# Shift products of two modulated norms: the shift held still, rounded weights of two tiles moved past it

## The chip, the cores and the metric

The kernel runs on one core of a Trainium2 chip (trn2). The time is device time in microseconds for one execution of the whole program, from its first to its last instruction on the core, as the median of the executions shown.

## What is computed

The reference runs two blocks, one behind the other, on a sequence of 512 rows with 1,024 features. The first has four layers: forgetting attention, a state-space layer, a multi-scale pool and again forgetting attention, each with a gated feed-forward net (SwiGLU). The second block has two layers with a mixer that joins attention and a state-space scan, and again a SwiGLU net. What the change touches is how the second block normalizes:

```
mod = (silu(c) @ w_ada[l] + b_ada[l])[:, None, :]
sh1, sc1, g1, sh2, sc2, g2 = jnp.split(mod, N_MOD, axis=-1)
h = rmsnorm(x, norm1_w[l]) * (1.0 + sc1) + sh1
x = x + g1 * hybrid_mixer(h, ...)
h = rmsnorm(x, norm2_w[l]) * (1.0 + sc2) + sh2
x = x + g2 * swiglu_2(h, w_gate_up[l], w_down[l])
```

So a product `h @ W` behind such a norm has two parts: the scaled `x` times `W`, which needs a factor for each row (the reciprocal root of the mean square), and the shift `sh` times `W`, one number for each column of `W`, the same for all rows.

## The kernel before

Activations are kept with the features on the partitions: `x` is eight tiles (`KD`) of 128 features x 512 rows. A weight tile is 128 x 128 and is the stationary operand, 512 rows move past it. Each fp32 value is split into two roundings of the type fp32r, a high and a low part (`Xh`, `Xl` for activations, `wh`, `wl` for weights), and a product is three matmuls: high by high, and the two mixed ones (`p3`, L265).

**Weights.** They lie in HBM in the order of use, eight tiles to a chunk of 128 x 1024. `pump` (L200) loads a chunk into `wraw` (four buffers, SyncE's queue), ScalarE rounds it into `wh` (three buffers, L174) and VectorE makes `wl` (two buffers, L181). `wnext(n, ...)` (L231) hands out the next n tiles of the current chunk; `raw_w` (L252) gives the unrounded fp32 tile.

**The order of work.** Each engine runs its instructions in an order that is laid down when the program is built: an instruction is placed when the model of the machine used there has its inputs and its buffers ready, those written first in the program going first. `keep_in_program_order` holds an instruction behind what was written before it for the same engine. Tiles of one tag share a fixed number of buffers.

**The modulation.** In the background of earlier layers the vector `mod` (128 x 96, both layers and all six parts) is made, and from it the gains `acol`; `end` (L1475) closes that work. `Ada` (L1493) is one modulated norm. There are four: the two mixers (`mixer`) and the two feed-forward nets (`feed`), in the order mixer 0, feed 0, mixer 1, feed 1. They are called lead 1 to lead 4 below.

**The lead** (L1537). The root of the mean square isn't known yet when a stage begins, so its first two weight tiles for each k, i = 0 and 1, are multiplied with `x` times gain, without the row factor, into `pld` (three matmuls each). Behind each of these, one fp32 product of the raw weight tile with one column, the shift, goes into `psh`; the two `psh` take both buffers of the PSUM tag `sc`. At k = 1 and k = 4 the sums of squares (`pc`, L401) and the row factors (`nps`, L411) are put in. At the end ScalarE copies the two columns into `adb` (`b`), and for every k VectorE makes `sqt` (x times gain times row factor; two buffers), ScalarE rounds `sqt` plus the shift into the new `Xh`, and VectorE makes the new `Xl`.

**Behind the lead** the other products use these new tiles: in the feed-forward net (`ffn7`, L670) the loop over k for `pgu`, in the mixer (`hybrid`, L1623) the loop for `pk` and `pm`, two weight tiles for each k. Only then is `pld` closed: times the row factor, plus `b`.

Of the kernel before, what the change touches and what calls it, by code (L numbers as in the profile page):

```python
# [20 lines left out]
P = 128  # L21
# [47 lines left out]
def kernel(  # L69
# [179 lines left out]
        pump(i)  # L249
        return hs[i], ls[i]  # L250

    def raw_w():  # L252

        c, o = divmod(st["slot"] - 1, SLOTS)
        return raws[c][:, o * P:(o + 1) * P]

    def walign(n):
        while st["slot"] % n:
            keys.append(None)
            st["slot"] += 1  # L260

    def mm(o, l, r, s0, s1, onto=False):
        pe.matmul(o, lhsT=l, rhs=r, start=s0, stop=s1, skip_group_check=onto)  # L263

    def p3(o, l, r, first, last, onto=False):  # L265
        mm(o, l[0], r[0], first, False, onto)
# [166 lines left out]
    def ffn(name_gu, name_dn, lay, deferred, post, nbg=3, lead=None, ada=None):  # L433
        with tc.tile_pool(name="ffn", bufs=1, reuse_waits="tile") as fp:
            ph = fp.tile([P, KF, S], F32R, name="ph")
            F0 = 3
            plo = [fp.tile([P, F0, S], F32R, name="pl0")]
            R = {}

            def pl(f):  # L440
                if f >= F0 and len(plo) == 1:
                    plo.append(fp.tile([P, KF - F0, S], F32R, name="pl1", tag="pl1", bufs=1))
                return plo[0][:, f, :] if f < F0 else plo[1][:, f - F0, :]

            def tmp():
                return fp.tile([P, S], F32, name="t1", tag="t1", bufs=3)

            def close(f, pg, pu):
                t_ = tmp()
                if deferred:  # L450
                    v.tensor_tensor(out=t_, in0=pg, in1=R["r"], op=ALU.mult)  # L451
                    a.activation(t_, t_, AF.Silu)
                    v.tensor_tensor(out=t_, in0=pu, in1=t_, op=ALU.mult)  # L453
                    g_.tensor_tensor(out=t_, in0=t_, in1=R["r"], op=ALU.mult)  # L454
                else:
                    a.activation(t_, pg, AF.Silu)
                    v.tensor_tensor(out=t_, in0=pu, in1=t_, op=ALU.mult)
                keep(f, t_)

            def keep(f, t_):  # L460
                a.activation(ph[:, f, :], t_, AF.Copy)
                v.tensor_tensor(out=pl(f), in0=t_, in1=ph[:, f, :].bitcast(F32), op=ALU.subtract)
                bgstep(nbg)

            def gu_key(which, f, k):
                return ("t", name_gu, lay, k * P, which * DFF + f * P)

            def gu(t, which, f, k):
                p3(t, wnext(1, gu_key(which, f, k)), xk(k), k == 0, k == KD - 1)

            f0 = 0
            if ada:
                f0 = 2
                (pg, pu), r, b = ada.lead([lambda k, i=i: gu_key(i, 0, k) for i in range(2)])
                pp = [acc("pgu") for _ in range(2)]
                for k in range(KD):
                    for i, t in enumerate(pp):
                        gu(t, i, 1, k)
                t_, tu = tmp(), tmp()
                tt(t_, pg, r, ALU.mult)  # L480
                a.activation(t_, t_, AF.Silu, bias=b[:, 0:1])
                tt(tu, pu, r, ALU.mult)
                stt(t_, tu, b[:, 1:2], t_, ALU.add, ALU.mult)
                keep(0, t_)
                close(1, *pp)
            if lead:

                f0 = F0
                steps = lead(fp.tile([P, (KF - F0) * S], F32, name="lroom", tag="pl1", bufs=1), tmp)
                pp = [(acc if i < 4 else scp)("pgu") for i in range(2 * f0)]  # L490
                for k in range(KD):
                    steps[k]()
                    for i, t in enumerate(pp):
                        gu(t, i % 2, i // 2, k)
                        if (k, i) == (KD - 1, 3):
                            rc = rstd_cols(nrm["sq"])
                R["r"] = keep_rstd(rstd_rows(rc))
                for f in range(f0):
                    close(f, pp[2 * f], pp[2 * f + 1])
            for f in range(f0, KF):  # L500
                pg, pu = acc("pg"), acc("pu")
                for which, t in enumerate((pg, pu)):
                    for k in range(KD):
                        gu(t, which, f, k)
                    if deferred and "c" not in R and not lead:
                        R["c"] = rstd_cols(nrm["sq"])
                    elif deferred and "r" not in R:
                        R["r"] = keep_rstd(rstd_rows(R["c"]))
                close(f, pg, pu)
            for m in range(KD):  # L510
                po = acc("po")
                for f in range(KF):
                    w = wnext(1, ("t", name_dn, lay, f * P, m * P))
                    p3(po, w, (ph[:, f, :], pl(f)), f == 0, f == KF - 1)
                post(m, po)
                bgstep(nbg)

    def ffn7(name_gu, name_dn, lay, deferred, upd, fin, nbg=3, ada=None, plain=(0,)):
# [4 lines left out]
        with tc.tile_pool(name="ffn", bufs=1, reuse_waits="tile") as fp:  # L523
# [41 lines left out]
            def gu_key(which, f, k):  # L565
                return ("t", name_gu, lay, k * P, which * DFF + f * P)
# [100 lines left out]
            f0 = 0  # L667
            if ada:
                f0 = 2
                (pg, pu), r, b = ada.lead([lambda k, i=i: gu_key(i, 0, k) for i in range(2)])  # L670
                pp = [acc("pgu") for _ in range(2)]
                for k in range(KD):
                    for i, t in enumerate(pp):
                        gu(t, i, 1, k)
                t_, tu = tmp(), tmp()
                tt(t_, pg, r, ALU.mult)
                a.activation(t_, t_, AF.Silu, bias=b[:, 0:1])
                tt(tu, pu, r, ALU.mult)
                stt(t_, tu, b[:, 1:2], t_, ALU.add, ALU.mult)
                keep(0, t_)  # L680
                close(1, *pp)
# [759 lines left out]


    mod = cp.tile([P, 96], F32, name="mod")
    acol = cp.tile([P, 32], F32, name="acol")

    def modc(lay, which, k):
# [3 lines left out]
    def ada_thunks(bp):  # L1450
# [24 lines left out]
        def end():  # L1475
            p2 = part.rearrange("p (i two) -> p two i", two=2)
            tt(mod, p2[:, 0], p2[:, 1], ALU.add)
            at, n_ = COLS["b_ada"]
            tt(mod, mod, cols[:, at:at + n_], ALU.add)
            for lay in range(2):  # L1480
                for i, nm in ((0, "n1"), (1, "n2")):
                    at, _ = COLS[nm]
                    sc = mod[:, lay * 48 + (1 + 3 * i) * 8:lay * 48 + (1 + 3 * i) * 8 + 8]
                    o = acol[:, lay * 16 + i * 8:lay * 16 + i * 8 + 8]
                    stt(o, sc, 1.0, cols[:, at + lay * 8:at + lay * 8 + 8], ALU.add, ALU.mult)
            at, n_ = COLS["fin_g"]
            tt(facol, acol[:, 0:KD], cols[:, at:at + n_], ALU.mult)

        return [start, act] + [lambda i=i: step(i) for i in range(192)] + [end] + rope_thunks(bp, T)
# [3 lines left out]
    class Ada:  # L1493
# [42 lines left out]

        def lead(self, keyf):  # L1537
            pp = [acc("pld") for _ in range(2)]
            pb = [scp("psh") for _ in range(2)]
            for k in range(KD):  # L1540
                for i in range(2):
                    w = wnext(1, keyf[i](k))
                    p3(pp[i], w, xk(k), k == 0, k == KD - 1)
                    mm(pb[i][:, 0:1], raw_w(), self.shift(k), k == 0, k == KD - 1)
                if k == AT_C:
                    rc = self.cols()
                if k == AT_R:
                    r = rstd_rows(rc)
            b = nsmall("adb", 2, 2)
            for i in range(2):  # L1550
                a.activation(b[:, i:i + 1], pb[i][:, 0:1], AF.Copy)
            for k in range(KD):
                xh, xl = new_X(k)
                u_ = ntile("sqt", 2)
                stt(u_, x[:, k, :], self.gain(k), r, ALU.mult, ALU.mult)
                a.activation(xh, u_, AF.Identity, bias=self.shift(k))
                stt(xl, u_, self.shift(k), xh.bitcast(F32), ALU.add, ALU.subtract)
            return pp, keep_rstd(r), b

        def final_x(self, k):  # L1560
            if k == 0:
# [30 lines left out]
    def hybrid(lay, post, ada):  # L1592
        W = "w_in_2"
        with tc.tile_pool(name="hyb", bufs=1, reuse_waits="tile") as fp:
# [25 lines left out]

            sql = []
            keyf = [lambda k, i=i: ("t", W, lay, k * P, i * P) for i in range(3)]
            pq, r, b = ada.lead(keyf[:2])  # L1623
            pk, pm = acc("pa"), acc("pm")
            for k in range(KD):
                p3(pk, wnext(1, keyf[2](k)), xk(k), k == 0, k == KD - 1)
                w = wnext(1, ("c", W, lay, k * P, ((0, 384, 32), (32, 1952, 8))))
                p3(pm[:64], [t_[:, :64] for t_ in w], xk(k), k == 0, k == KD - 1)
            for i in range(3):
                wcol = col("qa_w", 2 * lay + i) if i < 2 else col("kva_w", lay)  # L1630
                h_, l_ = (qn[0][:, i, :], qn[1][:, i, :]) if i < 2 else kvn
# [585 lines left out]
```

## Time and profile before

| | |
|---|---|
| median of 3 executions | 3480.41 us (3479.81 to 3483.42) |
| profiled execution, its own time | 3482.38 us |
| span of the profiled execution | 3480.6 us |
| TensorE (PE) matmul busy | 3412.9 us, 98% of the span |
| TensorE weight loads (PEld) busy | 2908.2 us, 84% |
| VectorE (DVE) busy | 2337.6 us, 67% |
| ScalarE (ACT) busy | 1486.0 us, 43% |
| GpSimd (POOL) busy | 486.6 us, 14% |
| mean granted TensorE clock | 0.992 |

Times in the trace count from the start of the span. Matmuls are pipelined: the record of one is longer than the spacing to the next, so what one costs in a stream is read from the distance between starts. Weight loads have records of their own. A row with x2 is two instructions merged; what stands in brackets is how long the engine stood idle before the row, and what it was released by. The lines of the code are given as L263 and the like; nearly all matmuls are issued by the helper in line 263, so they are told apart by the names of their tiles.

### The profile page before, as it was taken

The numbers are of one execution on the slowest core, as the hardware profiler recorded it, in microseconds if no ns is written. First come the engines' busy times: TensorE is split into PE (matmuls) and PEld (weight loads), VectorE is DVE, ScalarE is ACT, GpSimd is POOL, SyncE is SP. The second block draws the span as 40 slices with busy tenths as digits, with TensorE's granted clock in tenths as the row PEclk, the third lists the DMA queues.
The fourth block names the chain that finished last, engine by engine and source line by source line (L and its number), as shares of the span: only waits on it lengthen the run. The fifth ranks groups of instructions, "written<-read, shape, count | busy, mean of one in ns | idle before, by whom it ended". The sixth has DMA issues, their size and how long they took to land.

```text
span 3480.6 us, 49473 instructions
## 1 busy us (share of the span) xinstructions
PE 3412.9 (98%) x18620; PEld 2908.2 (84%) x18620; DVE 2337.6 (67%) x4335; ACT 1486.0 (43%) x2419; POOL 486.6 (14%) x597
## 2 busy tenths in 40 slices
PE   8999999989999989999999999999999999999999
PEld 6888778878888868888788989988889998788998
DVE  8876786355555576555676866876686677658666
ACT  4554333314433233322455633556553356645333
POOL 1003443011111021101000100132110002211000
PEclk9999999999999999999999999999999999999999
DMA  5423344474455434554422232321122232113232
GB/s 155 110 70 98 117 138 139 140 251 136 131 169 169 152 106 160 169 168 146 136 73 70 92 103 97 106 80 55 37 95 100 97 110 83 48 41 106 85 110 97
DMA packets 189167, 395.56 MB, mean 114 GB/s; under 512 B 57552, under 2 KB 84320, under 8 KB 186880
## 3 DMA queue, kind: packets, MB, share of 16 engines
q1 hardware_dynamic: 186592, 375.61, 33.3%
q10 hardware_dynamic: 2304, 16.78, 1.4%
q8 instruction: 146, 2.39, 0.3%
q14 instruction: 93, 0.76, 0.1%
q0 software_dynamic: 32, 0.02, 0.0%
HBM read 372.33 MB, written 24.20 MB: 114 GB/s over the span
## 4 chain that ended last, share of the span: by engine, by line
PE 70%; DVE 5%; ACT 2%; issue 1%; DMA 1%; POOL 1%; POOLq 0%; SPq 0%; DVEq 0%; ACTq 0%
PE po L263 20%; PE qa L263 9%; PE pu L263 8%; PE pg L263 7%; PE qc L263 7%; PE pgl L263 2%; PE px L263 2%; PE pq L263 2%; PE pv L263 2%; PE sc L263 2%; PE pld L263 1%; PE pz L263 1%; DVE wl L181 1%; PE tp L753 1%; PE pV L263 1%
## 5 line engine op out<-in xcount | busy, mean ns | idle before, releaser
L174 ACT ACTIVATE wh<-wraw 128x1024 fp32r<-128x1024 f32 x514 | 542.7, 1057 | 676.8 <-PE po L263 339.5
L181 DVE TENSOR_TENSOR wl<-wraw,wh 128x1024 fp32r<-128x1024 f32 x433 | 546.1, 1262 | 278.7 <-issue 81.2
L263 PE MATMUL po<-ph,wl 128*128 128x512 f32 x1056 | 411.0, 389 | 1.0 <-DVE wl L181 1.0
L263 PE MATMUL po<-ph,wh 128*128 128x512 f32 x1056 | 411.2, 390 | 0.0
L263 PE MATMUL po<-pl,wh 128*128 128x512 f32 x1056 | 411.0, 389 | 0.0
L390 POOL TENSOR_TENSOR sqa<-sqa,sqt 128x512 f32<-128x512 f32 x72 | 112.1, 1557 | 1390.3 <-ACT sqt L389 1389.7
L263 PE MATMUL pu<-Xh,wh 128*128 128x512 f32 x632 | 248.4, 393 | 0.0
L263 PE MATMUL pu<-Xh,wl 128*128 128x512 f32 x632 | 247.6, 392 | 0.6 <-DVE wl L181 0.6
L263 PE MATMUL pu<-Xl,wh 128*128 128x512 f32 x632 | 247.8, 392 | 0.2 <-DVE Xl L399 0.2
L263 PE MATMUL qa<-T,wh 128*128 128x256 f32 x1296 | 236.9, 283 | 0.0
L263 PEld LDWEIGHTS po<-ph,wl 128*128 128x128 f32 x1056 | 198.3, 188 | 42.8 <-DVE wl L181 1.4
L263 PEld LDWEIGHTS po<-pl,wh 128*128 128x128 f32 x1056 | 198.3, 188 | 41.2 <-DVE pl L551 0.4
L263 PEld LDWEIGHTS po<-ph,wh 128*128 128x128 f32 x1056 | 198.3, 188 | 41.0 <-issue 0.4
L263 PE MATMUL pg<-Xh,wh 128*128 128x512 f32 x568 | 223.7, 394 | 1.4 <-DVE t L451 1.4
L263 PE MATMUL pg<-Xl,wh 128*128 128x512 f32 x568 | 221.9, 391 | 0.0
L263 PE MATMUL pg<-Xh,wl 128*128 128x512 f32 x568 | 221.4, 390 | 0.0
L263 PEld LDWEIGHTS qa<-T,wh 128*128 128x128 f32 x1296 | 202.2, 192 | 0.0
L263 PE MATMUL qa<-T,wsl 128*128 128x256 f32 x648 | 183.8, 284 | 2.6 <-DVE wsl L181 2.6
L174 ACT ACTIVATE wh<-ws 128x1024 fp32r<-128x1024 f32 x108 | 114.4, 1059 | 151.6 <-PE po L263 48.4
L1471 DVE SCALAR_TENSOR_TENSOR adaj<-adaw,cbc 128x512 bf16<-128x512 f32 x192 | 143.7, 749 | 47.0 <-DMA adaw<-in_wada_dram 46.5
L181 DVE TENSOR_TENSOR wsl<-ws,wh 128x1024 fp32r<-128x1024 f32 x108 | 131.9, 1231 | 32.8 <-ACT wh L174 32.3
L454 POOL TENSOR_TENSOR t<-t,rstd 128x512 f32<-128x512 f32 x66 | 86.7, 1315 | 474.3 <-DVE t L453 471.6
(565 smaller groups left out, 8228.5 us busy)
## 6 DMA issues: line engine op xcount, KB each, us to landing
wraw<-in_wst_dram SPq DMA_DIRECT2D x541, 512.0 KB, 3.4
adaw<-in_wada_dram SPq DMA_DIRECT2D x192, 256.0 KB, 3.1
cbc<-c_d SPq DMA_DIRECT2D x32, 256.0 KB, 3.3
tbbr<-br_d ACTq DMA_DIRECT2D x8, 1024.0 KB, 5.5
tbct<-ct_d ACTq DMA_DIRECT2D x8, 1024.0 KB, 5.2
ct_d<-s5cp SPq DMA_DIRECT2D x128, 32.0 KB, 1.9
br_d<-s5ev SPq DMA_DIRECT2D x32, 128.0 KB, 2.0
ct_d<-kp_d SPq DMA_DIRECT2D x32, 128.0 KB, 2.8
```

The lines of the kernel that those rows point to most:

```text
L174: a.activation(hs[i], whole(i), AF.Copy)
L181: v.tensor_tensor(out=ls[i], in0=whole(i), in1=hs[i].bitcast(F32), op=ALU.subtract)
L263: pe.matmul(o, lhsT=l, rhs=r, start=s0, stop=s1, skip_group_check=onto)
L390: (v if m == KD - 1 else g_).tensor_tensor(out=nrm[key], in0=nrm[key], in1=q, op=ALU.add)
L454: g_.tensor_tensor(out=t_, in0=t_, in1=R["r"], op=ALU.mult)
L753: pe.transpose(t_[:, j * P:(j + 1) * P], pr[:, j * P:(j + 1) * P], ident)
L1471: tc.keep_in_program_order(v.scalar_tensor_tensor(out=j, in0=T.pop(i), scalar=1.0, in1=T["c"][:, (i % 2) * W:(i % 2) * W + W], op0=ALU.mul ...
```

## The change

The shift itself is split into two roundings, once, into `mods` (128 x 96 x 2). In the lead both weight tiles of a k are now taken together (`wnext(2, ...)`, with `walign(2)` ahead so that both lie in one chunk). The pair of roundings of the shift for this k, 128 x 2, becomes the stationary operand, and the rounded weights of the two tiles move past it, 256 columns at a time: once `wh`, once `wl`, all summed in the first two partitions of a single `psh`. The sum over the two partitions for each column is the shift product, but it lies along a row. It is copied into a buffer of the tag `sqt` (`rows_`), and `bias` turns it: two fp32 products, each with 2 x 128 values of `rows_` as the stationary operand and a column of two ones moving, into `psb`, then one copy into `adb`. `bias` is called behind k = 1 of the next loop, and its two products are held in that place by `here`. `raw_w` goes away.

```
+    mods = cp.tile([P, 96, 2], F32R, name="mods")
...
+            a.activation(mods[:, :, 0], mod, AF.Copy)
+            tt(mods[:, :, 1], mod, mods[:, :, 0].bitcast(F32), ALU.subtract)
...
         def lead(self, keyf):
             pp = [acc("pld") for _ in range(2)]
-            pb = [scp("psh") for _ in range(2)]
+
+            pb = scp("psh")
+            walign(2)
             for k in range(KD):
+                w = wnext(2, *[f_(k) for f_ in keyf])
                 for i in range(2):
-                    w = wnext(1, keyf[i](k))
-                    p3(pp[i], w, xk(k), k == 0, k == KD - 1)
-                    mm(pb[i][:, 0:1], raw_w(), self.shift(k), k == 0, k == KD - 1)
+                    p3(pp[i], tuple(t[:, i * P:(i + 1) * P] for t in w), xk(k), k == 0, k == KD - 1)
+                at = self.lay * 48 + self.i * 24 + k
+                for i in range(2):
+                    mm(pb[0:2, 0:2 * P], mods[:, at, :], w[i], k == 0 and i == 0, k == KD - 1 and i == 1)
                 if k == AT_C:
                     rc = self.cols()
                 if k == AT_R:
                     r = rstd_rows(rc)
             b = nsmall("adb", 2, 2)
-            for i in range(2):
-                a.activation(b[:, i:i + 1], pb[i][:, 0:1], AF.Copy)
+            rows_ = ntile("sqt", 2)
+            a.activation(rows_[0:2, 0:2 * P], pb[0:2, 0:2 * P], AF.Copy)
+
+            def bias():
+                p_ = scp("psb")
+                for i in range(2):
+                    here(mm(p_[:, i:i + 1], rows_[0:2, i * P:(i + 1) * P], ones[0:2, 0:1], True, True))
+                a.activation(b, p_[:, 0:2], AF.Copy)
+                return b
+
...
-            return pp, keep_rstd(r), b
+            return pp, keep_rstd(r), bias
```

In `ffn7` and `hybrid` the loop over k behind the lead gets, the same in both:

```
+                    if k == 1:
+                        b = bias()
```

New helpers are `here`, which is `tc.keep_in_program_order`, and `mm` now returns its instruction.

## Rows read from the trace of the kernel before

**Rows 1.** The page: busy time of TensorE, and the chain that ended last.
```profile
PE 3412.9 (98%) x18620; PEld 2908.2 (84%) x18620; DVE 2337.6 (67%) x4335; ACT 1486.0 (43%) x2419; POOL 486.6 (14%) x597
...
PE 70%; DVE 5%; ACT 2%; issue 1%; DMA 1%; POOL 1%; POOLq 0%; SPq 0%; DVEq 0%; ACTq 0%
```

**Rows 2.** View of the tile psh: record lengths min/median/max in ns, first and last start.
```profile
L263 PEld LDWEIGHTS psh<-mod,wraw x128: 187/188/338, 2269.6 to 3138.3; 128*128 128x128 f32 x128
L263 PE MATMUL psh<-mod,wraw x128: 164/228/353, 2269.8 to 3138.3; 128*128 128x1 f32 x128
L1551 ACT ACTIVATE adb<-psh x8: 152/171/172, 2290.2 to 3138.6; 128x1 f32<-128x1 f32 x8
```

**Rows 3.** Timeline of TensorE, lead 4 and behind it: start us, length us.
```profile
3122.06 0.39 PE L263 MATMUL pld<-Xh,wh 128*128 128x512 f32 x1
...
3122.74 0.28 PE L263 MATMUL psh<-mod,wraw 128*128 128x1 f32 x2
...
3132.93 0.47 PE L263 MATMUL pld<-Xh,wh 128*128 128x512 f32 x1
...
3138.42 0.48 PE L263 MATMUL pgu<-Xh,wh 128*128 128x512 f32 x1
...
3149.96 0.39 PE L263 MATMUL pg<-Xh,wh 128*128 128x512 f32 x1
```

**Rows 4.** Timeline, 256-column products in the feed-forward net behind lead 2.
```profile
2576.62 0.28 PE L263 MATMUL qc<-T,wsl 128*128 128x256 f32 x1
...
2578.05 0.28 PE L263 MATMUL qc<-T,wsl 128*128 128x256 f32 x1
```

**Rows 5.** Timeline of VectorE and ScalarE, end of lead 4 and behind it.
```profile
3133.21 1.41 DVE L281 SCALAR_TENSOR_TENSOR sqt<-x,acol,nps 128x512 f32<-128x512 f32 x2 [1.73 <-PE nps L263]
...
3133.99 1.38 ACT L1556 ACTIVATE Xh<-sqt,mod 128x512 fp32r<-128x512 f32 x2 [2.90 <-DVE sqt L281]
...
3134.75 1.42 DVE L281 SCALAR_TENSOR_TENSOR Xl<-sqt,mod,Xh 128x512 fp32r<-128x512 f32 x2
...
3136.08 1.40 DVE L281 SCALAR_TENSOR_TENSOR sqt<-x,acol,nps 128x512 f32<-128x512 f32 x2
...
3137.68 0.17 ACT L1551 ACTIVATE adb<-psh 128x1 f32<-128x1 f32 x1 [2.31 <-PE psh L263]
...
3138.49 1.22 DVE L181 TENSOR_TENSOR wl<-wraw,wh 128x1024 fp32r<-128x1024 f32 x1 [1.00 <-PE pld L263]
...
3139.63 1.49 DVE L281 SCALAR_TENSOR_TENSOR Xl<-sqt,mod,Xh 128x512 fp32r<-128x512 f32 x2
...
3141.03 1.40 DVE L281 SCALAR_TENSOR_TENSOR sqt<-x,acol,nps 128x512 f32<-128x512 f32 x2
...
3142.95 1.41 DVE L281 SCALAR_TENSOR_TENSOR Xl<-sqt,mod,Xh 128x512 fp32r<-128x512 f32 x2
```

**Rows 6.** Timeline of TensorE behind lead 4: two matmuls that waited.
```profile
3147.53 0.50 PE L263 MATMUL pgu<-Xl,wh 128*128 128x512 f32 x1 [0.22 <-DVE Xl L281]
...
3176.21 0.39 PE L263 MATMUL qc<-T,wsl 128*128 128x256 f32 x1 [1.22 <-DVE wsl L181]
```

**Rows 7.** One stretch of lead 1: length, busy us of PE, PEld, DVE, ACT, POOL, granted clock, DMA.
```profile
2276.30:2283.00 6.70, 6.70 (x22) 5.64 (x22) 0.72 (x1) 1.47 (x3) 1.17 (x4) 0.51 0.00 0
```

**Rows 8.** Timeline of TensorE in lead 1, at and behind the sums of squares.
```profile
2274.09 1.05 PE L263 MATMUL pc<-ones,sqa 128*128 128x1 f32 x8 [1.26 <-DVE sqa L390]
...
2275.55 0.95 PE L263 MATMUL pc<-ones,sq2a 128*128 128x1 f32 x8
...
2277.20 0.77 PE L263 MATMUL pld<-Xh,wh 128*128 128x512 f32 x1
...
2278.62 0.42 PE L263 MATMUL psh<-mod,wraw 128*128 128x1 f32 x2
2278.90 0.77 PE L263 MATMUL pld<-Xh,wh 128*128 128x512 f32 x1
```

**Rows 9.** View of the tile p1g: a ScalarE copy of 256 columns out of PSUM.
```profile
L638 ACT ACTIVATE p1g<-qa x27: 358/383/387, 1949.8 to 3425.2; 128x256 f32<-128x256 f32 x27
```

More of the change, by code (lines that the diff above doesn't have):

```diff
@@ L250, in quad_next @@
         return hs[i], ls[i]
-    def raw_w():
-        c, o = divmod(st["slot"] - 1, SLOTS)
-        return raws[c][:, o * P:(o + 1) * P]
     def walign(n):
@@ L262, in mm, with here @@
     def mm(o, l, r, s0, s1, onto=False):
-        pe.matmul(o, lhsT=l, rhs=r, start=s0, stop=s1, skip_group_check=onto)
+        return pe.matmul(o, lhsT=l, rhs=r, start=s0, stop=s1, skip_group_check=onto)
+    def here(ins):
+        return tc.keep_in_program_order(ins)
     def p3(o, l, r, first, last, onto=False):
@@ L473, in ffn @@
                 f0 = 2
-                (pg, pu), r, b = ada.lead([lambda k, i=i: gu_key(i, 0, k) for i in range(2)])
+                (pg, pu), r, bias = ada.lead([lambda k, i=i: gu_key(i, 0, k) for i in range(2)])
                 pp = [acc("pgu") for _ in range(2)]
@@ L669, in ffn7 @@
                 f0 = 2
-                (pg, pu), r, b = ada.lead([lambda k, i=i: gu_key(i, 0, k) for i in range(2)])
+                (pg, pu), r, bias = ada.lead([lambda k, i=i: gu_key(i, 0, k) for i in range(2)])
                 pp = [acc("pgu") for _ in range(2)]
@@ L674, in ffn7 @@
                         gu(t, i, 1, k)
+                    if k == 1:
+                        b = bias()
                 t_, tu = tmp(), tmp()
@@ L1622, in hybrid @@
             keyf = [lambda k, i=i: ("t", W, lay, k * P, i * P) for i in range(3)]
-            pq, r, b = ada.lead(keyf[:2])
+            pq, r, bias = ada.lead(keyf[:2])
             pk, pm = acc("pa"), acc("pm")
@@ L1628, in hybrid @@
                 p3(pm[:64], [t_[:, :64] for t_ in w], xk(k), k == 0, k == KD - 1)
+                if k == 1:
+                    b = bias()
             for i in range(3):
```

## The prediction

> **What bounds the kernel now.** I read the page first. TensorE is busy 98% of the span and makes up 70% of the chain that ended last [rows 1], so a matmul taken away normally gives its time back; the question is where something else ends last. The view of the tile `psh` then shows the whole of what is changed: 64 fp32 products recorded as 128 weight loads and 128 one-column matmuls, spread over four leads, and eight small copies into `adb` [rows 2]. Next comes TensorE in order of time through one lead (lead 4, the last feed-forward one). The reader is to see two spacings there: 0.68 us for the three 512-column products of a weight tile, and 0.915 us from one tile to the next [rows 3]. Then VectorE in the same lead, which makes the new `Xh`, `Xl` for the loop behind it [rows 5], and the places further on where TensorE waits for VectorE [rows 6]. Leads 2 and 3 repeat lead 4's spacings; lead 1 is different [rows 7, 8].
>
> **What a shift product costs.** Six tiles of lead 4, from 3132.93 to 3138.42, take 5.49 us, so 0.915 us each. Three 512-column matmuls take 0.68 us (3122.06 to 3122.74). The shift product is the rest, 0.235 us, and 16 of them make 3.76 us of a lead [rows 3].
>
> **What takes its place.** For every tile there is one 256-column product with a two-column stationary operand. No row has that stationary width. The nearest rows are 256-column products with full 128-column weights: twelve of them from 2576.62 to 2578.05, 0.119 us each [rows 4]. Upper bound: 0.119 us, since narrower weights can't load slower. Lower bound: half of a 512-column spacing of 0.227 us, 0.113 us. I take 0.119. Per lead, 16 x (0.235 - 0.119) = 1.86 us is saved; by the lower bound it would be 1.95 us.
>
> The Trainium skill (TensorE: Matmul & The Clock Gate, section Back-to-back issue gap) gives the isolated gap at full clock as N/2.4 + 2.5 ns, which is an estimate of 109 ns for 256 columns. The rows have 119 ns for that width, so the page's figure is below what this kernel shows; by it a lead would save 2.0 us instead of 1.86.
>
> **Lead 1.** Here TensorE is through its first four tiles at 2272.83 and then waits 1.26 us for VectorE's last square [rows 8]. The four tiles become 0.47 us faster and the wait 0.47 us longer: nothing gained. Behind it the clock is granted at 0.51, the lower of its two levels (1.2 of 2.4 GHz), for 6.7 us [rows 7]; a tile takes 1.70 us there, 2277.20 to 2278.90, of which the shift product's record is 0.42 us [rows 8]. Twice 0.119 us, an estimate, replaces that, leaving 1.52 us. Twelve tiles remain: before, 6.7 us hold 3.94 of them and 8.06 follow at 0.915, 14.07 us; after, 6.7 us hold 4.41 and 7.59 follow at 0.80, 12.77 us. Lead 1 saves 1.30 us if the clock does the same again.
>
> Gross: 1.30 + 3 x 1.86 = 6.88 us.
>
> **Does the saving get past VectorE?** Behind a lead VectorE ends last. In lead 4 it makes four `sqt` and two `Xl` by 3137.49, stands still 1.00 us until the lead's last `pld` lets go of a `wl` buffer, makes `wl` at 3138.49, and then runs `Xl` and `sqt` without a break [rows 5]; TensorE catches up with it at 3147.53 [rows 6]. So that run starts with the end of the lead, and an earlier end moves all of it forward, as long as VectorE's idle 1.00 us isn't used up. The six tiles behind `nps` shorten by 6 x 0.116 = 0.70 us, so it is not. What shifts the other way: the last reader of that `wl` buffer used to be `pld`, with the copy starting 0.07 us behind the lead's end (3138.49 against 3138.42). Now it is the last shift product. A 256-column matmul's record is about 0.28 us long and starts 0.12 us before the end, so `wl` starts about 0.2 us behind it. That is 0.13 us for each lead, 0.5 us in all.
>
> **The turn of the rows.** ScalarE copies 2x256 values out of PSUM (a 128x256 copy takes 0.383 us [rows 9]; of the two small copies of 0.17 us one goes away [rows 2]), and two fp32 products with one column turn them, pinned behind the k = 1 products of the next loop. A `psh` product is the same form with more rows: 0.235 us each, 0.47 us for a lead, at least 0.28 us by the length of its record alone. The loop behind lead 4 is 48 products of 0.227 us, 10.88 us, but takes from 3138.42 to 3149.96, 11.54 us, as TensorE meets VectorE's late `Xl` [rows 3, 6]. Those 0.66 us cover the 0.47; with the cover gone it would cost 4 x 0.47 = 1.9 us. Behind lead 4 a longer wait for `wsl` follows, 1.22 us [rows 6], a second cover. Behind the pinned turn the whole product stream waits, so its input must be early: TensorE reaches it 12 products, 2.72 us, behind the lead.
>
> **The borrowed buffer.** The rows lie in one of the two `sqt` buffers, which VectorE's run needs in pairs [rows 5]. In lead 4 both hold values when the lead ends, and the first comes free with the first `Xl` behind `wl`, about 2.1 us later (3139.63 plus 0.75, and the 0.13 from above). Then the copy (0.38 us) ends near 2.5 us, the turn runs from 2.72 to 3.2 us, and the second `sqt` of the next pair, wanted at 3.3 us behind the lead's end (3141.03 plus one of two steps), just finds its buffer. I charge 0.1 us a lead, 0.4 us in all; if each pair missed by a full 0.7 us step it would be 2.8 us.
>
> **The rest.** `mods` adds one copy and one subtraction of 96 columns, once, each at most the 0.383 us of 256 columns [rows 9], under TensorE's work in the second attention; uncovered, 0.8 us. Raw weight buffers come free earlier, as no product reads them: that changes when loads start, and no wait for `wraw` stands in the leads' chain. There are no new transfers, and `walign(2)` adds no padding where slots are even.
>
> Sum: 6.88 - 0.5 - 0.4 = 6.0 us. The profiled execution took 3482.38 us, so 3476.4 us; it stands 2.0 us above the median of the runs shown, 3480.41, so the forecast for a median is 3474.4 us. A measurement of this kernel can tell about 0.2%, 7.0 us; the forecast is just inside that.
>
> **The rivals.**
> *The borrowed buffer holds up VectorE.* If the rows take their buffer before the run of `sqt` begins, each `sqt`, `Xh`, `Xl` goes one after the other: from 3133.21 to the end of the first `Xl`, 0.71 us behind 3134.75, is 2.25 us, against 1.41 us for a step in pairs [rows 5]. It holds until the turn, about 7.8 us in all, 3.5 steps instead of 5.5, less the idle 1.00 us: some 1.5 us a lead, 6 us, which eats the gain: 3480 us. For it: the rows are written down ahead of the run. Against: their copy can't be ready before the lead ends, and today's `adb` copy, written down ahead too, runs at 3137.68, behind the first `Xh` at 3133.99 [rows 5].
> *TensorE stands at the turn (the other side).* If the copy gets its buffer only when the next pair's first `Xl` is done (3142.95 plus 0.71, 5.2 us behind the lead [rows 5]), the pinned turn would stop TensorE from 2.72 to 5.6 us, 2.9 us a lead; less the 0.66 us cover, 9 us over four, against 6.4 gained: 3483 us, and up to 3489 if the 1.22 us wait for `wsl` [rows 6] grows in each lead too. It decides from 2.2 us of standing a lead, 6.0 / 4 + 0.66. Against it: a turn that is late when the order is laid down can be placed behind later products, as only earlier ones are pinned ahead of it.
> *The clock.* The low clock in lead 1 comes behind the 1.26 us wait and 16 one-column matmuls [rows 7, 8]. Denser products might keep it at full: 6.7 us at half speed give back about 3.3 us, 3471 us. The wait grows by 0.47 us, which speaks for no change or worse (another 3.3 us, near 3478 us).
> The Trainium skill (TensorE: Matmul & The Clock Gate, section Why this matters for your kernels) asks that idle gaps between bursts of matmuls be kept short; by that the longer wait speaks against the change, and the low clock behind the wait agrees with it.
>
> **How the numbers follow.** Forecast 0.60; buffer 0.16; TensorE at the turn 0.10; clock regained 0.14. The forecast's own range is 3472 to 3478 us, by the unknown widths (+0.4), the turn's cover (-1.9), the buffer (-2.4) and 2 us by which runs differ. The threshold is 3473.4 us: of the forecast about a third lies below it, of the regained clock nearly all, 0.33 faster. Slower needs 3487.4 us: a third of the turn rival, and an order downstream that comes out badly, 0.07. The rest, 0.60, is within 0.2%. The range of 3469.5 to 3481.5 us leaves out the far ends of the clock and the turn.
>
> **What would show it.** No `psh` record with one column; 64 of 128x256 with a 0.119 us spacing; tiles 0.80 us apart; leads of 14.5 us instead of 16.36 (3122.06 to 3138.42); `wl` 0.2 us behind a lead's end; the turn inside the next loop, which stays at about 11.5 us. Wrong would be: a TensorE wait ended by ScalarE's copy ahead of the turn, `sqt` going singly, or a change in the stretches between leads, where nothing is edited and only the order could differ.

## The result, and the profile after

The changed kernel takes 3505.7 us in the median (3499.4 to 3509.7, 6 executions); the kernel before took 3478.2 us on the same chip (3473.2 to 3483.4, 6). The ratio on record is 1.007, 95% interval [1.006, 1.0079]; the two medians alone give 1.0079. The forecast was 3474.4 us and the range ended at 3481.5: the change was to gain 6 us and loses 27.5 by the medians. The profiled execution after has a span of 3503.7 us, 23.1 us more than that of before.

The page of the kernel after shows nothing of it: TensorE's busy share and the head of the chain that ended last are those of [rows 1].

```profile
PE 3421.9 (98%) x18572; PEld 2899.6 (83%) x18572; DVE 2338.4 (67%) x4336; ACT 1489.5 (43%) x2420; POOL 481.3 (14%) x597
...
PE 70%; DVE 5%; ACT 2%; DMA 1%; issue 1%; POOL 1%; SPq 0%; DVEq 0%; ACTq 0%; POOLq 0%
```

The tile `psh` after, which answers to [rows 2]: 64 products with 256 columns and two-column weights in place of 64 recorded in 128 pieces, and one copy of 2 x 256 for each lead.

```profile
L258 PEld LDWEIGHTS psh<-wh,mods x32: 82/83/123, 2273.1 to 3155.3; 128*2 128x2 f32 x32
L258 PE MATMUL psh<-wh,mods x32: 277/280/345, 2273.3 to 3155.6; 128*2 128x256 f32 x32
...
L258 PE MATMUL psh<-wl,mods x32: 276/281/285, 2273.4 to 3155.7; 128*2 128x256 f32 x32
L1561 ACT ACTIVATE sqt<-psh x4: 357/357/358, 2292.2 to 3156.8; 2x256 f32<-2x256 f32 x4
```

TensorE in order of time at the end of lead 4, after; it answers to [rows 3] and [rows 6].

```profile
3154.18 0.39 PE L258 MATMUL pld<-Xh,wh 128*128 128x512 f32 x1
...
3155.57 0.28 PE L258 MATMUL psh<-wh,mods 128*2 128x256 f32 x1
3155.68 0.28 PE L258 MATMUL psh<-wl,mods 128*2 128x256 f32 x1
3158.75 1.06 PE L258 MATMUL pgu<-Xh,wh 128*128 128x512 f32 x2 [2.79 <-ACT Xh L1574]
...
3165.45 0.50 PE L258 MATMUL pgu<-Xl,wh 128*128 128x512 f32 x1 [0.84 <-DVE Xl L280]
...
3168.75 0.73 PE L258 MATMUL pgu<-Xh,wh 128*128 128x512 f32 x2 [0.71 <-ACT Xh L1574]
...
3170.07 0.50 PE L258 MATMUL pgu<-Xl,wh 128*128 128x512 f32 x1 [0.59 <-DVE Xl L280]
...
3174.22 0.50 PE L258 MATMUL pgu<-Xl,wh 128*128 128x512 f32 x1 [0.96 <-DVE Xl L280]
...
3176.60 0.39 PE L258 MATMUL pg<-Xh,wh 128*128 128x512 f32 x1
```

The products are as cheap as forecast: two tiles and their two shift products, 3154.18 to 3155.80 by the spacing of 0.12, take 1.62 us, 0.81 us a tile where it was 0.915. But behind the lead TensorE stands for 2.79 us, waits again and again for `Xh` and `Xl`, and the loop that took 11.54 us takes 17.85 (3158.75 to 3176.60). VectorE and ScalarE at the same place, after, which answers to [rows 5]:

```profile
3156.06 1.23 DVE L181 TENSOR_TENSOR wl<-wraw,wh 128x1024 fp32r<-128x1024 f32 x1 [6.23 <-PE psh L258]
3156.85 0.36 ACT L1561 ACTIVATE sqt<-psh 2x256 f32<-2x256 f32 x1
3157.20 0.74 DVE L280 SCALAR_TENSOR_TENSOR sqt<-x,acol,nps 128x512 f32<-128x512 f32 x1
3157.98 0.72 ACT L1574 ACTIVATE Xh<-sqt,mod 128x512 fp32r<-128x512 f32 x1 [0.77 <-DVE sqt L280]
3158.73 0.75 DVE L280 SCALAR_TENSOR_TENSOR Xl<-sqt,mod,Xh 128x512 fp32r<-128x512 f32 x1 [0.79 <-ACT Xh L1574]
...
3159.52 0.75 DVE L280 SCALAR_TENSOR_TENSOR sqt<-x,acol,nps 128x512 f32<-128x512 f32 x1
...
3163.35 0.60 PE L258 MATMUL psb<-ones,sqt 2*128 2x1 f32 x4
...
3163.99 0.17 ACT L1567 ACTIVATE adb<-psb 128x2 f32<-128x2 f32 x1 [0.45 <-PE psb L258]
3163.99 0.75 DVE L280 SCALAR_TENSOR_TENSOR sqt<-x,acol,nps 128x512 f32<-128x512 f32 x1 [0.61 <-PE psb L258]
```

Before, the first two `sqt` began at 3133.21, 5.2 us ahead of the lead's end [rows 5]. Now VectorE does nothing for the last 6.23 us of the lead; the first `sqt` comes at 3157.20, 1.2 us behind the record of the last shift product (3155.68 plus 0.28), and then one `sqt`, one `Xh`, one `Xl` take turns until the turn of the rows gives back the second buffer at 3163.99. The granted clock pays too. The windows of the same stretch (length; busy time of PE, PEld, DVE, ACT, POOL; granted clock; DMA):

```profile
3155.97:3158.75 2.78, 0.00 (x0) 0.00 (x0) 1.90 (x3) 1.96 (x3) 0.00 (x0) 1.00 0.19 31
3158.75:3161.75 3.00, 3.00 (x7) 2.12 (x8) 2.93 (x5) 0.72 (x1) 0.00 (x0) 0.54 0.38 146
3161.75:3176.60 14.85, 11.74 (x46) 7.84 (x45) 13.51 (x21) 8.81 (x13) 1.91 (x2) 0.98 0.11 35
```

In the 3.0 us behind the 2.79 us of standing the clock is granted at 0.54, near the lower of its two levels (1.2 of 2.4 GHz). The Trainium skill (TensorE: Matmul & The Clock Gate, section Why this matters for your kernels) asks that idle gaps between bursts of matmuls be kept short. The trace agrees in that the low clock comes behind the stand, though this stand of 2.79 us is shorter than the gaps that the page warns of.

The four leads side by side, from TensorE's starts: a lead from its first `pld` to the first product of the loop behind it, and that loop up to the first product of what follows. All in us, one profiled execution each; the last five rows are experiments below.

| | lead 1, loop | lead 2, loop | lead 3, loop | lead 4, loop | sum |
|---|---|---|---|---|---|
| before | 21.84, 12.33 | 16.36, 11.53 | 16.36, 11.49 | 16.36, 11.54 | 117.8 |
| after | 22.09, 16.68 | 18.40, 17.68 | 17.72, 16.03 | 18.40, 17.85 | 144.8 |
| own tile | 19.17, 11.75 | 15.49, 11.68 | 14.77, 11.75 | 15.44, 11.66 | 111.7 |
| rows behind the run | 19.17, 11.68 | 15.44, 11.66 | 14.77, 11.68 | 15.47, 11.71 | 111.6 |
| three buffers | 22.03, 15.07 | 18.41, 13.30 | 17.72, 13.45 | 18.41, 13.55 | 131.9 |
| turn not held | 22.11, 13.26 | 18.39, 14.05 | 17.74, 15.55 | 18.40, 14.05 | 133.6 |
| own tile but in lead 4 | 19.17, 11.75 | 15.45, 11.66 | 14.77, 11.75 | 18.40, 18.98 | 121.9 |

After against before, these stretches are 27.0 us longer. Lead 1 began 2.9 us later (2271.97 against 2269.12), ahead of which only the making of `mods` is edited (0.29 and 0.25 us, at 1717.9 and 1719.0) and executions differ by some us; the other stretches behind it gave 6.8 us back, which makes the 23.1 of the span. What came back lies in the two feed-forward nets, behind the loops of leads 2 and 4, which take 322.9 us up to lead 3 and 327.1 up to the end, in place of 326.3 and 330.7: TensorE's two waits for `wsl` in each (1.3 and 1.2 us, the second in [rows 6] for lead 4) are gone after. With the buffer borrowed in lead 4 alone (below) the stretch behind lead 4 takes 327.1 us, with four own tiles 330.0: some 3 us of a stand ahead of a feed-forward net come back in it.

### The profile page after: what moved, and what is told of

Read it like the earlier page. It is cut to its first block, busy times and chain, and to the rows that moved or that the text cites. A ratio compares the mean times of both kernels' runs of the same rounds, so it can differ in the third digit from the quotient of the medians.

```text
span 3503.7 us, 49376 instructions
## 1 busy us (share of the span) xinstructions
PE 3421.9 (98%) x18572; PEld 2899.6 (83%) x18572; DVE 2338.4 (67%) x4336; ACT 1489.5 (43%) x2420; POOL 481.3 (14%) x597
## 4 chain that ended last, share of the span: by engine, by line
PE 70%; DVE 5%; ACT 2%; DMA 1%; issue 1%; POOL 1%; SPq 0%; DVEq 0%; ACTq 0%; POOLq 0%
PE po L258 20%; PE qa L258 9%; PE pu L258 7%; PE qc L258 7%; PE pg L258 7%; PE pgl L258 2%; PE px L258 2%; PE pq L258 2%; PE pv L258 2%; PE sc L258 2%; PE pz L258 1%; PE tp L756 1%; PE pld L258 1%; DVE wl L181 1%; PE pV L258 1%
```

## The experiments

The theory formed from these rows, called the order theory: the buffers of a tag are handed out in the order in which the tiles are written in the program. `rows_` is written ahead of the eight `sqt`, and its copy can't be placed before the lead's last shift product; so every `sqt`, though its own inputs are ready in the middle of the lead, is placed behind it, and on VectorE behind the `wl` that waits for the lead's end. The rivals: two buffers are too few for nine tiles (capacity); the pinned turn stops TensorE (turn); the new products themselves.

**`rows_` in a tile of its own.**

```
-            rows_ = ntile("sqt", 2)
+            rows_ = cp.tile([P, 2 * P], F32, name="rows_", tag="shrow", bufs=1)
```

> The changed kernel, but the rows of the shift products get a buffer of their own (128 x 256) instead of one of the two sqt buffers; products, turn and its place stay. Order theory (the rows claim an sqt buffer first, so VectorE's run of sqt can't begin before their copy at the lead's end): the run begins ahead of the lead's end again, and the kernel takes 6 us less than before, about 3472 us if before takes 3478. Turn theory (TensorE stands at the pinned turn): the turn is where it was, so it stays some 27 us above before, near 3505 us. Product theory (the 256-column products with two-column weights are themselves dear): also near 3505 us.

Measured: 3472.55 us (11 executions), ratio to before 0.9981 [0.9972, 0.999]. The whole loss is gone and the forecast's gain is there. VectorE no longer stands through the lead's second half; its first `sqt` follows `nps`, as before the change:

```profile
3122.03 1.41 DVE L280 SCALAR_TENSOR_TENSOR sqt<-x,acol,nps 128x512 f32<-128x512 f32 x2 [1.28 <-PE nps L258]
```

The copy (into `rows__28828`, as the trace names the tile), written at the same place as in the changed kernel, now stands behind the second pair of `Xh` in ScalarE's order, so being written first holds up nothing by itself; it does so where the tag is shared:

```profile
3126.96 0.36 ACT L1561 ACTIVATE rows__28828<-psh 2x256 f32<-2x256 f32 x1
```

This doesn't yet tell order from capacity, as the tile gives the run both buffers as well.

**Three `sqt` buffers, `rows_` still in one of them.**

```
-            rows_ = ntile("sqt", 2)
+            rows_ = ntile("sqt", 3)
```

and the same at the two other places of the tag.

> The changed kernel with three sqt buffers instead of two, the rows still in one of them. Order theory: the copy of the rows must still get its buffer before the first sqt does, so VectorE still stands idle for 5 us or more at the end of every lead and the first sqt comes behind it; only the run's pairing comes back. I expect 10 to 18 us above before, 3488 to 3496 us. Capacity theory (all of the loss is that the run has one buffer instead of two while the rows hold the other): the run has its two, so about 6 us below before, 3472 us.

Measured: 3499.45 us (4 executions), ratio 1.0054 [1.0036, 1.0072]: far from the capacity theory's 3472, and 3.5 us above the end of the order theory's range. Two buffers are now always free for the run, and still it begins behind the lead. The timeline of VectorE and ScalarE in lead 4:

```profile
3149.89 1.23 DVE L181 TENSOR_TENSOR wl<-wraw,wh 128x1024 fp32r<-128x1024 f32 x1 [6.24 <-PE psh L258]
3150.73 0.36 ACT L1561 ACTIVATE sqt<-psh 2x256 f32<-2x256 f32 x1
3151.03 1.40 DVE L280 SCALAR_TENSOR_TENSOR sqt<-x,acol,nps 128x512 f32<-128x512 f32 x2
...
3152.58 1.22 PE L258 MATMUL pgu<-Xh,wh 128*128 128x512 f32 x2 [2.79 <-ACT Xh L1574]
```

The first `sqt` starts before the rows' copy ends (3150.73 plus 0.36), right at the end of `wl`: it waits for neither the copy nor a buffer, but for its place in VectorE's order. What capacity costs is seen behind it: the steps go in pairs again, the loops take 13.3 to 15.1 us in place of 16.0 to 17.9. In the table the third buffer takes 13 us off the sum, by the medians only 6. Most of the difference is lost again behind leads 2 and 4, where TensorE's waits for `wsl` are back (1.5 and 1.3 us each) and the nets take 326.7 and 330.8 us against 322.9 and 327.1 in the changed kernel.

**No hold on the turn.**

```
-                    here(mm(p_[:, i:i + 1], rows_[0:2, i * P:(i + 1) * P], ones[0:2, 0:1], True, True))
+                    mm(p_[:, i:i + 1], rows_[0:2, i * P:(i + 1) * P], ones[0:2, 0:1], True, True)
```

> The changed kernel with the turn of the rows no longer held behind k = 1 of the next loop; the rows stay in an sqt buffer. Turn theory: TensorE no longer stands at the turn, about 3472 us. Order theory: the turn goes up to the lead's end and the rows let go of their buffer early, so the run has pairs again, but it still starts only behind the lead: 8 to 18 us above before, 3486 to 3496 us.

Measured: 3502.72 us (4 executions), ratio 1.0067 [1.0053, 1.008], the changed kernel's within the interval: a miss for the turn theory and, by 6.7 us, for the order theory's range. Not pinned, the turn is placed directly behind the lead, and TensorE waits for it and for `Xh` in two pieces, in sum 2.18 us in lead 4 in place of 2.79:

```profile
3158.73 0.60 PE L258 MATMUL psb<-ones,sqt 2*128 2x1 f32 x4 [1.29 <-ACT sqt L1561]
...
3160.22 1.22 PE L258 MATMUL pgu<-Xh,wh 128*128 128x512 f32 x2 [0.89 <-ACT Xh L1574]
```

VectorE still stands 6.23 us, so the hold is not the cause. But it has a share: without it the run goes in pairs again, as forecast, and the table's sum is 11 us smaller. The time doesn't show it. In the profiled execution the nets behind leads 2 and 4 take 327.7 and 330.3 us, as TensorE waits there again (2.7 us each), and the stretch behind lead 3 takes 222.1 us at a granted clock of 0.98, in place of 217.5 at 1.00. What lowered the clock there, and whether the other executions have it, isn't shown.

**The old products, with a borrowed buffer.** The kernel before, with its fp32 products and without a turn; only the two columns of `psh` go through a buffer of `sqt` written ahead of the run, and from there into `adb` behind k = 1 of the loop.

```
             b = nsmall("adb", 2, 2)
+            rows_ = ntile("sqt", 2)
             for i in range(2):
-                a.activation(b[:, i:i + 1], pb[i][:, 0:1], AF.Copy)
+                a.activation(rows_[:, i:i + 1], pb[i][:, 0:1], AF.Copy)
...
+            def bias():
+                a.activation(b, rows_[:, 0:2], AF.Copy)
+                return b
```

> The kernel before with its old one-column fp32 products, and one thing of the change alone: the two shift columns are copied into an sqt buffer written down ahead of the run of sqt, and from there into adb; no turn. Order theory: VectorE's run starts behind the lead's end, as in the changed kernel, though the buffer comes free at once: 10 to 18 us above before, 3488 to 3496 us. Product theory and turn theory: neither new products nor turn are in it, so the same as before, 3478 us.

Measured: 3494.34 us (5 executions), ratio 1.0042 [1.0028, 1.0057]: a loss of the same kind with none of the new products. The timeline of lead 4 also shows how fine the order is. Here the first column of `psh` is final a tile ahead of the lead's end, and just one `sqt` is placed in front of `wl`; the next stands behind it.

```profile
3135.56 0.75 DVE L281 SCALAR_TENSOR_TENSOR sqt<-x,acol,nps 128x512 f32<-128x512 f32 x1 [1.73 <-PE nps L263]
3140.09 0.17 ACT L1556 ACTIVATE sqt<-psh 128x1 f32<-128x1 f32 x1 [6.65 <-PE psh L263]
...
3140.89 1.23 DVE L181 TENSOR_TENSOR wl<-wraw,wh 128x1024 fp32r<-128x1024 f32 x1 [4.59 <-PE pld L263]
```

**The rows behind the run.** The one thing moved in the changed kernel is where `rows_` is written; two buffers, borrowing and turn stay.

```
-            rows_ = ntile("sqt", 2)
-            a.activation(rows_[0:2, 0:2 * P], pb[0:2, 0:2 * P], AF.Copy)
...
             for k in range(KD):
                 xh, xl = new_X(k)
...
+            rows_ = ntile("sqt", 2)
+            a.activation(rows_[0:2, 0:2 * P], pb[0:2, 0:2 * P], AF.Copy)
             return pp, keep_rstd(r), bias
```

> The changed kernel with one thing moved: rows_, still in one of the two sqt buffers, is taken and copied behind the loop that makes the eight sqt, not ahead of it. Order theory (the run of sqt must wait because rows_ was written ahead of it in the same two buffers): the run starts inside the lead again, the loops behind the leads go back to about 11 to 12 us, and the time is near that of the run with rows_ in its own tile, 3470 to 3476 us. Capacity theory (two buffers are too few for nine tiles, wherever the ninth stands): the last steps of the run go singly, 1 to 3 us a lead, 3476 to 3484 us. Turn theory (the pinned products stop TensorE): the copy comes later than before, so the stop grows, 3510 us or more.

Measured: 3472.08 us (10 executions; the kernel before on this chip 3483.18), ratio 0.9973 [0.9962, 0.9984]. Same buffers, same products, two lines written later: from 0.7% slower to 0.27% faster. This is the run that tells order from capacity, and turn from both, since the copy comes later than in the changed kernel. What a trace shows is the order on the engines; that the hand-out of the buffers makes this order is read from which edits undo it. The timeline of lead 4:

```profile
3121.38 1.41 DVE L280 SCALAR_TENSOR_TENSOR sqt<-x,acol,nps 128x512 f32<-128x512 f32 x2 [1.30 <-PE nps L258]
...
3128.81 1.22 DVE L181 TENSOR_TENSOR wl<-wraw,wh 128x1024 fp32r<-128x1024 f32 x1
...
3134.56 0.37 ACT L1575 ACTIVATE sqt<-psh 2x256 f32<-2x256 f32 x1 [0.23 <-DVE Xl L280]
...
3135.27 0.60 PE L258 MATMUL psb<-ones,sqt 2*128 2x1 f32 x4
```

VectorE begins its run inside the lead, `wl` comes later without a wait, and the rows' copy takes the buffer that the run no longer needs, 8.5 us behind the lead's end at 3126.05. The turn lands late in the loop, and TensorE's matmuls show no idle time ahead of it.

**Borrowing in lead 4 alone.** Leads 1 to 3 with a tile of their own.

```
-            rows_ = ntile("sqt", 2)
+            rows_ = ntile("sqt", 2) if self.lay and self.i else cp.tile([P, 2 * P], F32, name="rows_", tag="shrow", bufs=1)
```

> The changed kernel with rows_ in a tile of its own in leads 1 to 3 and in an sqt buffer in lead 4 alone. Order theory, a loss made separately by each lead: a quarter of the distance between the changed kernel (3505.7 us) and the one with four own tiles (3472.55 us), 8.3 us, so 3481 us (3478 to 3484), with leads 1 to 3 and their loops as in the latter. Rival (the new buffer moves other things in memory or in the order laid down far from the leads, and the own tile repaired that): 3473 us or 3500 us, nothing in between.

Measured: 3482.04 us (10 executions), ratio 1.0001 [0.9987, 1.0015]. From 0.9981 with four own tiles to 1.007 with none is 0.0089; a quarter of it on top of 0.9981 is 1.0003. The table has the loss where the buffer is borrowed and nowhere else: 37.38 us for lead 4 and its loop against 27.10 with its own tile.

**Own tile and three buffers.** The edits of the first two experiments together; `rows_` has the tile of its own.

> rows_ in a tile of its own and three sqt buffers in place of two. Order theory: nothing holds up the run any more, and TensorE sets the loops' end but for the small waits for Xl; a third buffer lets VectorE run one step further ahead of ScalarE, 0 to 2 us in all: 3470 to 3474 us. Capacity theory (buffers are what is short): 4 us or more faster than with two, 3468 us or less.

Measured: 3480.45 us (10 executions), ratio 0.9997 [0.9985, 1.0008]. A miss for both theories by the time. The leads and loops sum to 110.0 us, 1.7 less than with two buffers, and all of that in lead 1 (17.56 against 19.17), where the clock is granted in full (the row stands with the clock of lead 1 below); the other three gain nothing. So the third buffer speeds up no run that isn't held up, as the order theory has it.

What is lost lies elsewhere. Against the kernel with the rows behind the run, whose profiled execution is 12.0 us shorter, lead 1 begins 6.1 us later (2271.36 against 2265.26), and the stretches behind leads 1 and 3 take 219.3 and 222.1 us at granted clocks of 0.99 and 0.98 in place of 217.7 and 217.5 at 1.00. The tag also serves the squares of every norm (L387), and in the first 40 us of the program the two kernels with three buffers start fewer matmuls than the seven others: 90 here and 89 where the rows borrow, against 109 to 119. First the row with own tile and three buffers, then that with the rows behind the run:

```profile
0.00:40.00 40.00, 25.55 (x90) 20.21 (x91) 22.16 (x88) 20.21 (x28) 11.24 (x16) 0.87 0.55 183
```

```profile
0.00:40.00 40.00, 28.92 (x119) 22.22 (x120) 26.54 (x102) 24.22 (x34) 13.06 (x16) 1.00 0.60 197
```

That this start makes the 8 us between the medians isn't shown: in the changed kernel, with two buffers, lead 1 begins as late (2271.97). The cause stays open.

## Why the prediction was wrong, step by step

**The step that failed: the borrowed buffer.** It was charged 0.1 us a lead. By the medians, own tile against shared buffer is 3472.55 against 3505.7 us, 33 us or 8.3 us a lead. The working started from [rows 5], "In lead 4 both hold values when the lead ends, and the first comes free with the first `Xl` behind `wl`", and asked only when a buffer comes free on the chip. It didn't ask who is handed a buffer first when the order is laid down. `rows_` is written first, so the buffers that held `sqt` values during the lead hold none now.

**The first rival had the condition, and only the smaller part of the mechanism.** "If the rows take their buffer before the run of `sqt` begins" came true, and until the turn the steps do go singly. Its 1.5 us a lead counted single steps against paired ones, from the place where the run begins today (and two steps of 1.41 less 1.00 are 1.8, not 1.5). The run doesn't begin there: VectorE stands from the middle of the lead (6.23 us) and the whole run starts some 6.5 us later against the lead's end (5.2 us ahead of it before, over 1.2 behind it after). The Trainium skill (PSUM — Partial Sum Buffer, section Engine vs sequencer instructions) says that VectorE's queue is strictly first in, first out; the row agrees, as `sqt`, whose inputs are there, stays behind a `wl` that waits 6.23 us.

The price of lead 4, 36.25 us against 27.18 with the rows behind the run, is 9.1 us. It is read from the distance between starts, as a record is longer than the spacing: TensorE stands 2.95 us from the lead's end (3155.80) to 3158.75, where the bracket shows 2.79. The four later waits take 4.1 us, where the brackets show 3.10; from 3168.75 to 3170.07, for one, two products take 1.32 us in place of 0.45. The clock takes 1.7 us, 3.0 us at 0.54 and 14.85 us at 0.98. That leaves 0.3 us.

The reason given against this rival, that "today's `adb` copy, written down ahead too, runs at 3137.68, behind the first `Xh`", was true and beside the point. `adb` had a tag of its own, so nothing stood in line behind its copy. `rows_` stood in the line of VectorE's run.

**What held.** With the buffer out of the way a gain near the forecast's own 6.0 us is there: 5.6 us by the medians with an own tile, and 6.1 us in the stretches of the table. But the terms behind it were off in both directions, and that they meet near 6 is in part luck (1.6 us by the clock of lead 1):

- The product: 0.12 us forecast and measured, 0.81 us a tile where 0.80 was said.
- Leads 2 to 4: 1.86 us each forecast. With an own tile lead 3 gains 1.59, leads 2 and 4 only 0.87 and 0.92. There TensorE now arrives at the sums of squares before VectorE has the last square, as was said for lead 1 alone; this row of lead 4 with an own tile has no counterpart before:

```profile
3115.77 1.05 PE L258 MATMUL pc<-ones,sqa 128*128 128x1 f32 x8 [0.42 <-DVE sqa L389]
```

- Lead 1: 1.30 us forecast, 2.67 measured. The wait for the square did grow, from 1.26 to 1.45 us, by less than the 0.47 said. Behind it 4.1 us at a clock of 0.58 (the first window below) stand in place of 6.7 us at 0.51 [rows 7]: 1.7 us given up instead of 3.3, a difference of 1.6 us, without which lead 1 gains 1.1. That the denser products did this, as the rival on the clock has it, isn't shown. With the old products (the kernel with a borrowed buffer) the low clock behind the same wait is just as short, and with own tile and three buffers there is none, behind a wait of 1.40 us; one execution of each kernel was profiled.

With an own tile:

```profile
2271.50:2275.60 4.10, 4.10 (x17) 3.22 (x17) 0.90 (x5) 1.74 (x3) 2.83 (x10) 0.58 0.34 120
2275.60:2284.80 9.20, 9.20 (x49) 6.95 (x49) 5.83 (x10) 3.58 (x6) 0.11 (x1) 1.00 0.19 59
```

With the old products and a borrowed buffer, the wait and the low clock behind it:

```profile
2269.56 1.05 PE L263 MATMUL pc<-ones,sqa 128*128 128x1 f32 x8 [1.25 <-DVE sqa L390]
...
2272.40:2275.80 3.40, 3.40 (x12) 2.83 (x12) 0.00 (x0) 0.00 (x0) 0.53 (x2) 0.50 0.00 0
```

With own tile and three buffers, the wait and all of lead 1:

```profile
2276.15 1.05 PE L258 MATMUL pc<-ones,sqa 128*128 128x1 f32 x8 [1.40 <-DVE sqa L389]
...
2271.36:2288.92 17.56, 16.16 (x89) 12.44 (x88) 11.70 (x21) 10.23 (x15) 6.00 (x12) 1.00 0.30 103
```

- The turn: four records, 0.60 us, 0.47 forecast, hidden as said: the loops with an own tile take 11.66 to 11.75 us against 11.49 to 12.33 before, and TensorE waits for nothing in the loop behind lead 4.
- `wl` later by 0.13 us a lead, 0.5 us in all: not seen as a cost. With an own tile it is placed further back in VectorE's order and waits for nothing there.

**The second rival** expected TensorE to stand at the turn. It stands, but at the first product of the loop, for `Xh`; without the hold the time is the same. Its longer wait for `wsl` didn't come either: that wait is gone.

## What to carry to other kernels

When a new tile shares a tag with a run of others, ask where it is written and when its input is ready: one tile whose input comes late, written ahead of a run that is ready early, holds up the whole run, here with three buffers as with two. Write it behind the run, or give it a tag of its own; both cost nothing here and turn +0.7% into -0.2 to -0.3%. And price a rival from the place where its mechanism bites first, not from where the work stands today.

## What the runs showed of the hardware

A stand of TensorE of 2.79 us behind a lead was followed by 3.0 us at a granted clock of 0.54. Behind the wait for the square in lead 1 the low clock came out differently from kernel to kernel: 6.7 us at 0.51 before the change (a wait of 1.26 us) [rows 7, 8], 4.1 us at 0.58 with an own tile (1.45 us), 3.4 us at 0.50 with the old products and a borrowed buffer (1.25 us), and none with own tile and three buffers (1.40 us). So the length of the wait doesn't give the length of the low stretch, and one profiled execution doesn't tell what an edit did to it. A 256-column product with weights of two columns has the same spacing, 0.12 us, as one with 128 columns of weights, 0.119 us [rows 4]; its weight load's record is shorter, 0.083 us against 0.188 us for the 128-column fp32 load of [rows 2].
